# A decoder block's output projection: its weights split into DRAM during the first projection

## The chip, the cores and the metric

The kernel runs on one core of a Trainium2 chip, in float32. The metric is the device time of one launch in microseconds. A core has a matrix engine (TensorE, PE), a vector engine (VectorE, DVE), a scalar engine (ScalarE, ACT), a general engine (GpSimd, POOL) and a sync engine (SyncE, SP), each with its own instruction stream that it works through in order. SP, ACT and POOL issue DMAs. On chip there are SBUF (128 partitions) and PSUM, where matmuls accumulate. The engines wait for each other by semaphores.

## The reference, cut to what matters

One layer over 2048 tokens of width 1024: a norm, one combined projection, stick-breaking attention over 8 heads and gated linear attention (GLA) over 4, head norms, an output projection with a residual, and a feed-forward block (FFN) with a convolution of width 3 and a final norm.

```
h = rms_norm(x, attn_norm_g)
proj = h @ w_in                       # 1024 x 3088
sb_q, sb_k, sb_v, g_q, g_k, g_v, g_lr, g_og = split(proj)
o_sb = head_rms_norm(stick_breaking_attention(sb_q, sb_k, sb_v), sb_out_g)
log_a = log_sigmoid(g_lr @ w_gate_up + b_gate_up) / 16
o_gla = head_rms_norm(gla_chunked(g_q, g_k, g_v, log_a), gla_out_g) * silu(g_og)
x = x + concat([o_sb, o_gla]) @ w_out # 1024 x 1024
h = rms_norm(x, ffn_norm_g)
a, val = split(causal_depthwise_conv(h @ w_ffn_up, conv_w, conv_b))
x = x + (silu(a) * val) @ w_ffn_down
return rms_norm(x, final_norm_g)
```

## The kernel before

The tokens go in four blocks of 512. Every float32 matmul is made of three matmuls in a reduced format: each operand is kept as a high part and a low part (value minus high part), and high x high, high x low and low x high are accumulated. `split_w` (L101) makes the two parts of weights: ACT copies into the high part (L102), POOL or DVE subtracts it for the low part (L103).

The first stage is the projection of the GLA values (`gv_block`, L183) beside the norm of x (`prep`, L193): `prep(b + 1)` and then 4 token tiles of block b, 24 matmuls each. The weights of a projection come in four loads (`load_chunk`, L147) into two buffers `raw` and four pairs `w`. The second stage projects the GLA's queries, keys and gate: for each block the low-rank gate `lr` (two ACT copies, L250 and L251, and one subtract, L252), one matmul with `gu` for each pair of heads (L257) and 24 matmuls for each of the four feature tiles (`mm_feat`, L163). The gate's small operands are loaded in front of it, in L221 to L239. Then follow Q, K, V with the GLA itself, the output gate and attention. Up to the output gate the order of all engines is made by a scheduler with a timeline model of the engines; from there on the order of PE is written out by hand, and the others are scheduled around it.

The output projection and the FFN's down projection run in one generator, `accumulate` (L733): for n = 0, 1 (columns 0 to 511, then 512 to 1023) it takes chunks of 128 rows of the weights, each with 4 token tiles of 3 matmuls (L764 to L766). `load` (L746) brings a chunk: for block 0 a raw 256 KB load by SP, the split, and a 512 KB store of the pair by POOL to DRAM (`wou` for the output projection, `wdn` for the down projection); the later blocks load the pair from there (512 KB). For n = 0 of block 0 it takes its buffers from `ahead` (L690), four raw buffers and four pairs in slots 10, 11 and 14 of the big memory that come free at the end of the attention of the first block; otherwise from `dr`, a ring of three pairs. Beside the first output projection, attention of the next block runs (`z`, `ws`, `acc`), and the first FFN weights come in (`uraw`).

Of the kernel before, what the change touches and what calls it, by code (L numbers as in the profile page):

```python
# [8 lines left out]
F32 = mybir.dt.float32  # L9
F32R = mybir.dt.float32r  # L10
# [40 lines left out]
def hybrid_block_kernel(ctx, tc, x, attn_norm_g, w_in, w_gate_up, b_gate_up, sb_out_g,  # L51
# [60 lines left out]
    def slot(n, shape, dtype, name):  # L112
        return big.tile(shape, dtype, tag=f"slot{n}", name=name)
# [4 lines left out]
    if True:  # L118
# [54 lines left out]
        def mm_tok(w, b, t):  # L173
            ps = mm_ps()
            whi, wlo = w
            ts = slice(t * P, (t + 1) * P)
            for k in range(KT):
                nc.tensor.matmul(ps, hh[b][k // 4][:, k % 4, ts], whi[k], start=(k == 0), stop=False)  # L178
                nc.tensor.matmul(ps, hh[b][k // 4][:, k % 4, ts], wlo[k], start=False, stop=False)  # L179
                nc.tensor.matmul(ps, hl[b][k // 4][:, k % 4, ts], whi[k], start=False, stop=(k == KT - 1))  # L180
            return ps

        def gv_block(w, b):  # L183
            for t in range(4):
                ps = mm_tok(w, b, t)
                gt = ev.tile([P, 2, TB], F32, tag="ev", name="gt")[:, 0]
                nc.scalar.activation(gt, ps, AF.Copy)
                nc.sync.dma_start(out=gvs[b][t * P:(t + 1) * P, :], in_=gt)

        with tc.tile_pool(name="xp", bufs=2, side="right") as xp, tc.tile_pool(name="sm", bufs=2, side="right") as sm:  # L190
            gat = m1_tile([P, D], F32, "gat")

            def prep(b):  # L193
                for t in range(4):
                    xt = xp.tile([P, D], F32, tag="xt", name="xt")
                    r0 = b * TB + t * P
                    nc.sync.dma_start(out=xt, in_=x[r0:r0 + P, :])
                    if r0 == 0:
                        nc.scalar.dma_start(out=gat, in_=attn_norm_g.to_broadcast([P, D]))
                    xn = xp.tile([P, D], F32, tag="xn", name="xn")  # L200
                    ss = sm.tile([P, 1], F32, tag="ss", name="ss")
                    nc.scalar.activation(xn, xt, AF.Square, accum_out=ss)
                    r = rstd_of(sm, ss, D, 1, "n")
                    nc.vector.scalar_tensor_tensor(out=xn, in0=xt, scalar=r, in1=gat, op0=ALU.mult, op1=ALU.mult)
                    for k4 in range(2):
                        tp = pt.tile([P, 4, P], F32, tag="tp", name="tp")
                        for kk in range(4):
                            k = 4 * k4 + kk
                            nc.tensor.transpose(tp[:, kk, :], xn[:, k * P:(k + 1) * P], ident)
                        dh = hh[b][k4][:, :, t * P:(t + 1) * P]  # L210
                        dl = hl[b][k4][:, :, t * P:(t + 1) * P]
                        split_psum(dh, dl, tp)

            prep(0)
            w = load_chunk(OFF_GV)
            for b in range(NB):
                if b + 1 < NB:
                    prep(b + 1)
                gv_block(w, b)

        nc.sync.dma_start(out=bgate, in_=b_gate_up.rearrange("o (j p) -> p (o j)", p=P))  # L221
        nc.sync.dma_start(out=g_o[:, 0:4], in_=sb_out_g.rearrange("o (j p) -> p (o j)", p=P))
        nc.sync.dma_start(out=g_o[:, 4:8], in_=gla_out_g.rearrange("o (j p) -> p (o j)", p=P))


        with tc.tile_pool(name="lr", bufs=2, side="right") as lp, tc.tile_pool(name="lc", bufs=1, side="right") as lc:
            lraw = lc.tile([P, KT, 16], F32, name="lraw")
            nc.sync.dma_start(out=lraw, in_=wv[:, :, OFF_LR:OFF_LR + 16])
            lw = lc.tile([P, KT, 2, 16], F32R, name="lw")
            split_w(lw[:, :, 0, :], lw[:, :, 1, :], lraw)  # L230

            gur = lc.tile([96, 256], F32, name="gur")
            for u in range(6):
                nc.sync.dma_start(out=gur[16 * u:16 * (u + 1), :], in_=w_gate_up)
            gu = lc.tile([96, 256], F32R, name="gu")
            nc.scalar.activation(gu, gur, AF.Copy)
            nc.vector.tensor_tensor(out=gu[64:96, :], in0=gur[64:96, :], in1=gu[64:96, :].bitcast(F32),
                                    op=ALU.subtract)
            mask = lc.tile([P, TB], F32, name="mask")  # L239
            nc.vector.memset(mask, 1.0)  # L240
            nc.vector.memset(mask.rearrange("p (n c) -> p n c", c=P)[:, :, 0:1], 0.0)
            w = load_chunk(OFF_GQK)
            for b in range(NB):
# [11 lines left out]
                for j in range(NPAIR):  # L255
# [38 lines left out]
                    nc.vector.tensor_tensor(out=ee, in0=pk, in1=ee, op=ALU.mult)  # L294
                    nc.sync.dma_start(out=gs[j][b][2], in_=ee)

        cg = ExitStack()
        gl = cg.enter_context(tc.tile_pool(name="gl", bufs=2, side="right"))
        gst = cg.enter_context(tc.tile_pool(name="gst", bufs=1, side="right"))
# [361 lines left out]
    for b in range(NB):  # L661
        for t in range(4):
            if (b, t) == (1, 0):
                tpc = pc.tile([P, 4, 2 * NCH], F32, tag="c", name="tpc")
                for k in range(4):
                    nc.tensor.transpose(tpc[:, k, :], crow[:, k, :], ident[0:2 * NCH, 0:2 * NCH])
                nc.vector.tensor_copy(out=cwb, in_=tpc)
            for part, _ in enumerate(og_group(b, t)):
                if b > 0:

                    if steps < (16 * (b - 1) + 4 * t + part + 1) * FIRST // 46:
                        next(first, None)
                        steps += 1
                    for f, when in enumerate(PAIRS):
                        if f not in oT and steps >= when:
                            oT[f] = o_feat(0, f, pc, "c")
                for f, row in GATED.items():
                    if f not in oT and (b, t) >= row:
                        oT[f] = o_feat(0, f, pc, "c", ot=ots[f % 4])
            if (b, t) == (1, 3):  # L680
                gring.items += gated_rows(0)
                a4 = slot(4, [P, 4, TB], F32, "wtC")
                w45 = slot(5, [P, 2, 2, TB], F32R, "ws45")
                wsr.items += [w45[:, 0], w45[:, 1]]
                ots = [a4[:, k, :].rearrange("p (t q) -> p t q", t=4) for k in range(4)]
            elif (b, t) == (2, 3):
                gring.items += gated_rows(1)
                wraw = slot(11, [P, 4, TB], F32, "wraw")
                wsplit = slot(10, [P, 4, TB], F32R, "wsplit")
    for _ in first:  # L690
        pass
    wmore = slot(14, [P, 4, TB], F32R, "wmore")
    ahead = [Ring([wraw[:, k, :] for k in range(4)]),
             Ring([m[:, 2 * u:2 * u + 2, :] for m in (wsplit, wmore) for u in range(2)])]
    del wsr.items[2:]
    c1.close()
    rings, o2 = later_memory(*shared[:-1], a4, shared[-1])
# [32 lines left out]
            dr.items += [m[:, 2 * u:2 * u + 2, :] for m in spare for u in range(2)]  # L730
        return True

    def accumulate(lhs, w_rows, kept, b, squares=None, extra=None, stagger=False, rstds=None, rows=None, first=None,  # L733
                   final=False):


# [3 lines left out]
        for n in range(2):  # L740
# [4 lines left out]

            def load(ci):  # L746
                at_ = kept[n][rows[ci]]
                pair = first[1].next() if n == 0 and first else dr.next()
                if b > 0:
                    nc.sync.dma_start(out=pair.bitcast(F32), in_=at_.bitcast(F32))  # L750
                else:
                    raw = first[0].next() if n == 0 and first else drr.next()
                    nc.sync.dma_start(out=raw, in_=w_rows[rows[ci] * P:(rows[ci] + 1) * P, ns])
                    split_w(pair[:, 0, :], pair[:, 1, :], raw, nc.vector if first and n == 0 and ci % 2 else nc.gpsimd)
# [62 lines left out]
    def ffn(b, oT, rows, nextT):  # L817
# [15 lines left out]
        if b == 0:  # L833
# [4 lines left out]
        r2 = sm.tile([P, 4], F32, tag="r2", name="r2", bufs=2)  # L838
        rs1, rs2 = ([r[:, t:t + 1] for t in range(4)] for r in (r1, r2))
        last = b + 1 == NB  # L840
        yield from accumulate(oT, w_out, wou, b, squares=sq1, stagger=True, rstds=[r1], rows=rows,
                              extra=previous if b > 0 else remaining, first=None if b > 0 else ahead)
        if b == 0:
            h2h.extend(slot(10 + u, [P, 4, TB], F32R, f"h2h{u}") for u in range(2))
# [24 lines left out]
        for gi, G in enumerate(GROUPS):  # L869
# [53 lines left out]
            yield from accumulate(gts, w_ffn_down[ch0 * P:(ch0 + G) * P, :], [w[ch0:ch0 + G] for w in wdn], b, squares=sq2 if final else None,  # L923
                                  extra=extra, stagger=final and last, rstds=[r2], final=final and last)
            ch0 += G
        while b + 1 < NB and len(nextT) < KT:
# [74 lines left out]
```

## Time and profile before

| | us |
|---|---|
| median of 3 runs | 2754.53 |
| lowest, highest | 2751.18, 2754.88 |
| the profiled execution, whole | 2760.47 |
| its span | 2758.8 |
| PE busy | 2694.3 |
| DVE, ACT, POOL busy | 1685.5, 1147.0, 611.6 |

The profiled execution is one launch of the same program, recorded by the hardware profiler. PE is busy for nearly all of the span, so its order of work is also the order of time: one reads where PE waits, for what, and then what the engine that it waits for was itself waiting for. A row in a timeline begins with the start and the duration, and the bracket at its end says how long the engine was idle before and what ended that.

### The profile page before, as it was taken

To read this page: it belongs to the slowest core of one execution; us is meant where nothing else is said; L and a number is where in the kernel's file an instruction comes from. 1 tells how busy PE (TensorE), PEld (TensorE's weight loads), DVE (VectorE), ACT (ScalarE), POOL (GpSimd) and SP (SyncE) were. 2 spreads that over 40 slices of the span, in tenths; PEclk is the share of its full clock that TensorE was granted. 3 is DMA by queue.
4 is the path that set the end of the run, shared out by engine and by line. 5 is a ranking of instruction groups with operands and counts; after the bars stand their busy time and mean duration, and the time that the engine had idled before them with its cause. 6 is when DMAs were issued, how large, how long until landed. Compare 5 with 4: busy or idle time off the path is not lost.

```text
span 2758.8 us, 36075 instructions
## 1 busy us (share of the span) xinstructions
PE 2694.3 (98%) x13004; PEld 2234.3 (81%) x13004; DVE 1685.5 (61%) x2778; ACT 1147.0 (42%) x2371; POOL 611.6 (22%) x937
## 2 busy tenths in 40 slices
PE   8999999999799999999999999999999999999998
PEld 7878888888688778887888888888888888888887
DVE  5246755467677687876776777777867334242333
ACT  5455533345465455554543444445434222220112
POOL 2001212215555556542111111111110000000000
PEclk9999999999999999999999999999999999999999
DMA  6214644467667677768455555574554656555552
GB/s 191 92 64 173 228 144 156 131 188 242 224 225 257 224 243 255 243 236 274 156 185 181 175 174 174 186 253 152 177 177 150 231 192 221 203 197 191 198 191 84
DMA packets 232169, 526.92 MB, mean 191 GB/s; under 512 B 32294, under 2 KB 120630, under 8 KB 209462
## 3 DMA queue, kind: packets, MB, share of 16 engines
q1 hardware_dynamic: 200742, 387.76, 42.3%
q0 software_dynamic: 31104, 136.33, 13.9%
q8 instruction: 102, 1.67, 0.3%
q14 instruction: 77, 0.63, 0.1%
q10 hardware_dynamic: 144, 0.52, 0.1%
HBM read 382.99 MB, written 141.56 MB: 190 GB/s over the span
## 4 chain that ended last, share of the span: by engine, by line
PE 86%; DVE 5%; DMA 4%; ACT 2%; issue 1%; POOL 1%; SPq 0%; ACTq 0%; POOLq 0%; DVEq 0%
PE ups L886 11%; PE ups L887 11%; PE ups L888 11%; PE d L765 7%; PE d L764 7%; PE d L766 7%; PE z L533 4%; PE tp L566 4%; PE mm L170 2%; PE mm L168 2%; PE mm L169 2%; PE acc L582 2%; PE mm L180 2%; PE mm L179 2%; PE mm L178 2%; PE acc L581 2%
## 5 line engine op out<-in xcount | busy, mean ns | idle before, releaser
L886 PE MATMUL ups<-h2h,u 128*128 128x512 f32 x1408 | 552.2, 392 | 3.9 <-DVE x L791 3.9
L887 PE MATMUL ups<-h2l,u 128*128 128x512 f32 x1408 | 551.1, 391 | 0.0
L888 PE MATMUL ups<-h2h,u 128*128 128x512 f32 x1408 | 550.3, 391 | 0.0
L886 PEld LDWEIGHTS ups<-h2h,u 128*128 128x128 f32 x1408 | 265.2, 188 | 60.6 <-DVE x L791 4.3
L95 DVE TENSOR_TENSOR ws<-tp,ws 128x512 fp32r<-128x512 f32 (+1 forms) x320 | 194.0, 606 | 193.2 <-ACT ws L94 192.3
L888 PEld LDWEIGHTS ups<-h2h,u 128*128 128x128 f32 x1408 | 265.0, 188 | 57.2
L887 PEld LDWEIGHTS ups<-h2l,u 128*128 128x128 f32 x1408 | 265.0, 188 | 55.4
L764 PE MATMUL d<-d,g 128*128 128x512 f32 x736 | 290.4, 395 | 3.8 <-ACT d L102 1.3
L94 ACT ACTIVATE ws<-tp 128x512 fp32r<-128x512 f32 (+1 forms) x320 | 170.3, 532 | 297.0 <-PE tp L566 292.8
L765 PE MATMUL d<-d,g 128*128 128x512 f32 x736 | 288.7, 392 | 1.2 <-POOL d L103 1.2
L766 PE MATMUL d<-d,g 128*128 128x512 f32 x736 | 288.4, 392 | 0.0
L898 DVE SCALAR_TENSOR_TENSOR ct<-ups,cwb,ct 128x511 f32<-128x511 f32 x176 | 131.7, 748 | 249.4 <-POOL ct L897 196.2
L893 ACT ACTIVATE ct<-ups,cwb 128x512 f32<-128x512 f32 x176 | 136.5, 775 | 340.0 <-PE ups L888 339.8
L549 DVE TENSOR_TENSOR_SCAN wtB<-mt,cy 128x512 f32<-128x512 f32 x192 | 249.0, 1297 | 4.4 <-ACT mt L538 4.3
L791 DVE TENSOR_TENSOR x<-d,x 128x512 f32<-128x512 f32 x128 | 85.8, 683 | 164.1 <-PE d L766 164.0
L897 POOL TENSOR_TENSOR ct<-ct,hadd 128x2 f32<-128x2 f32 x132 | 26.7, 202 | 688.5 <-ACT halo L895 324.3
L538 ACT ACTIVATE mt<-z 128x512 f32<-128x512 f32 (+2 forms) x320 | 170.6, 533 | 14.3 <-PE z L536 6.2
L764 PEld LDWEIGHTS d<-d,g 128*128 128x128 f32 x736 | 138.3, 188 | 35.3 <-DVE x L791 2.8
L765 PEld LDWEIGHTS d<-d,g 128*128 128x128 f32 x736 | 138.3, 188 | 31.2 <-POOL d L103 1.8
L766 PEld LDWEIGHTS d<-d,g 128*128 128x128 f32 x736 | 138.2, 188 | 30.8
L168 PE MATMUL mm<-hh,w 128*128 128x512 f32 x384 | 151.3, 394 | 0.0
L170 PE MATMUL mm<-hh,w 128*128 128x512 f32 x384 | 149.3, 392 | 0.9 <-POOL w L103 0.9
(265 smaller groups left out, 5374.2 us busy)
## 6 DMA issues: line engine op xcount, KB each, us to landing
u<-wup SPq DMA_DIRECT2D x132, 1024.0 KB, 4.7
d<-wdn SPq DMA_DIRECT2D x94, 512.0 KB, 3.5
wup<-u POOLq DMA_DIRECT2D x44, 1024.0 KB, 6.6
kvA<-kvs POOLq DMA_DIRECT2D x52, 512.0 KB, 4.6
uraw<-in_w_ffn_up_dram SPq DMA_DIRECT2D x44, 512.0 KB, 4.7
wdn<-d POOLq DMA_DIRECT2D x44, 512.0 KB, 4.9
d<-wou SPq DMA_DIRECT2D x38, 512.0 KB, 4.6
dw<-wdn SPq DMA_DIRECT2D x38, 512.0 KB, 4.3
```

Of the source, the lines that this page charges most:

```text
L94: nc.scalar.activation(hi, ps, AF.Copy)
L95: nc.vector.tensor_tensor(out=lo, in0=ps, in1=hi.bitcast(F32), op=ALU.subtract)
L168: nc.tensor.matmul(ps, whi[k][:, fs], hh[b][k // 4][:, k % 4, :], start=(k == 0), stop=False)
L170: nc.tensor.matmul(ps, wlo[k][:, fs], hh[b][k // 4][:, k % 4, :], start=False, stop=(k == KT - 1))
L538: nc.scalar.activation(m[:, lo:TB], z[:, :width], AF.Sigmoid, scale=-0.125)
L549: nc.vector.tensor_tensor_scan(out=pp[:, ::-1], data0=mr, data1=mr, initial=1.0 if prev is None else prev, op0=ALU.mult, op1=ALU.bypass)
L764: nc.tensor.matmul(accs[t], gh[:, ts], whi, start=(ci == 0), stop=False)
L765: nc.tensor.matmul(accs[t], gh[:, ts], wlo, start=False, stop=False)
L766: nc.tensor.matmul(accs[t], gw[:, ts], whi, start=False, stop=(ci == G - 1))
L886: nc.tensor.matmul(ps, whi[:, k, :], hk, start=(k == 0), stop=False)
L887: nc.tensor.matmul(ps, whi[:, k, :], lk, start=False, stop=False)
L888: nc.tensor.matmul(ps, wlo[:, k, :], hk, start=False, stop=(k == KT - 1))
```

## The change

`gv_block` gets a step of its own for each of its 16 token tiles, `split_ahead`: ACT issues a load of one 128 x 512 piece of `w_out` into `sraw` (a buffer in the tag `n2`, one copy), `split_w` makes the pair in `spair` (a pool `sp` with one buffer), and POOL issues its store into `wou`. The output projection of block 0 then loads pairs from `wou` as the others do: `ahead` becomes a ring of eight pairs in slots 10, 11, 14 and 15, and its own raw loads, splits and stores are gone. The gates' operands (`lraw`, `lw`, `gur`, `gu`, `bgate`, `g_o`) are loaded in the second round of the first stage, into a pool that is opened before it; the mask moves into the pool of the gate's working tiles, which is opened after `sp` is closed. By the addresses that the two programs were given, `spair` has bytes 196608 to 200703 of each partition, and later the mask has 196992 to 199039 and `lr` 199040 to 201087.

```diff
+        def split_ahead(raw, pair, src, dst):
+            nc.scalar.dma_start(out=raw, in_=src)
+            split_w(pair[:, 0, :], pair[:, 1, :], raw)
+            nc.gpsimd.dma_start(out=dst.bitcast(F32), in_=pair.bitcast(F32))
         def gv_block(w, b):
             for t in range(4):
+                i = 4 * b + t
+                split_ahead(n2_tile([P, 512], "sraw"),
+                            sp.tile([P, 2, 512], F32R, tag="spair", name="spair"),
+                            w_out[(i // 2) * P:(i // 2 + 1) * P, (i % 2) * 512:(i % 2 + 1) * 512], wou[i % 2][i // 2])
                 ps = mm_tok(w, b, t)
...
-        with tc.tile_pool(name="xp", bufs=2, side="right") as xp, tc.tile_pool(name="sm", bufs=2, side="right") as sm:
+        lc = cl.enter_context(tc.tile_pool(name="lc", bufs=1, side="right"))
+        lw = lc.tile([P, KT, 2, 16], F32R, name="lw")
...
+        def gate_operands():
+            nc.sync.dma_start(out=lraw, in_=wv[:, :, OFF_LR:OFF_LR + 16])
+            split_w(lw[:, :, 0, :], lw[:, :, 1, :], lraw)
+            for u in range(6):
+                nc.sync.dma_start(out=gur[16 * u:16 * (u + 1), :], in_=w_gate_up)
+            nc.scalar.activation(gu, gur, AF.Copy)
...
+        with tc.tile_pool(name="xp", bufs=2, side="right") as xp, tc.tile_pool(name="sm", bufs=2, side="right") as sm, \
+                tc.tile_pool(name="sp", bufs=1) as sp:
             gat = m1_tile([P, D], F32, "gat")
...
             for b in range(NB):
                 if b + 1 < NB:
                     prep(b + 1)
+                if b == 1:
+                    gate_operands()
                 gv_block(w, b)
-        with tc.tile_pool(name="lr", bufs=2, side="right") as lp, tc.tile_pool(name="lc", bufs=1, side="right") as lc:
-            lraw = lc.tile([P, KT, 16], F32, name="lraw")
...
-            mask = lc.tile([P, TB], F32, name="mask")
+        with tc.tile_pool(name="lr", bufs=2, side="right") as lp:
+            mask = lp.tile([P, TB], F32, tag="mask", name="mask", bufs=1)
...
-                wraw = slot(11, [P, 4, TB], F32, "wraw")
-                wsplit = slot(10, [P, 4, TB], F32R, "wsplit")
+                wsplit = [slot(n, [P, 4, TB], F32R, f"ws{n}") for n in (10, 11)]
     for _ in first:
         pass
-    wmore = slot(14, [P, 4, TB], F32R, "wmore")
-    ahead = [Ring([wraw[:, k, :] for k in range(4)]),
-             Ring([m[:, 2 * u:2 * u + 2, :] for m in (wsplit, wmore) for u in range(2)])]
+    wsplit += [slot(n, [P, 4, TB], F32R, f"ws{n}") for n in (14, 15)]
+    ahead = Ring([m[:, 2 * u:2 * u + 2, :] for m in wsplit for u in range(2)])
...
-                pair = first[1].next() if n == 0 and first else dr.next()
-                if b > 0:
+                pair = first.next() if n == 0 and first else dr.next()
+                if split:
                     nc.sync.dma_start(out=pair.bitcast(F32), in_=at_.bitcast(F32))
                 else:
-                    raw = first[0].next() if n == 0 and first else drr.next()
+                    raw = drr.next()
...
-        yield from accumulate(oT, w_out, wou, b, squares=sq1, stagger=True, rstds=[r1], rows=rows,
+        yield from accumulate(oT, w_out, wou, True, squares=sq1, stagger=True, rstds=[r1], rows=rows,
```

The order of ACT where the first projection ends and the second begins, before (`gt` is a result of `gv_block`, `w` a weight pair of the second projection; a name such as DMAHW2 or DMASW7 is a semaphore that DMAs count on, DMASW for those that POOL issues):

```order
L187 ACTIVATE gt_1097<-mm_1072 128x512 [waits DMAHW7_49,PE_49,Activation_49]
L102 ACTIVATE w_1159<-raw_1157 128x1024 [waits PE_49]
L102 ACTIVATE w_1164<-raw_1162 128x1024 [waits PE_49]
L187 ACTIVATE gt_1125<-mm_1100 128x512 [waits DMAHW0_49,PE_49,Activation_49]
L102 ACTIVATE w_1169<-raw_1167 128x1024 [waits DMAHW2_49]
L250 ACTIVATE lr_1194<-mm_1177 32x512 [waits DVE_49,PE_49]
L251 ACTIVATE lr_1194<-mm_1177 32x512
L102 ACTIVATE w_1174<-raw_1172 128x1024 [waits DMAHW3_49]
```

The same place of ACT now, from the last result of the first projection on:

```order
L197 ACTIVATE gt_1245<-mm_1220 128x512 [waits DMAHW5_49,PE_49]
L185 DMA sraw_1180<-in_w_out_dram 128x512 [waits Pool_49]
L102 ACTIVATE w_1269<-raw_1267 128x1024 [waits DMAHW0_49]
L102 ACTIVATE w_1274<-raw_1272 128x1024 [waits DMAHW1_49]
L102 ACTIVATE spair_1181<-sraw_1180 128x512 [waits DMAHW3_49,DMASW5_49]
L185 DMA sraw_1214<-in_w_out_dram 128x512 [waits Pool_49]
L102 ACTIVATE spair_1215<-sraw_1214 128x512 [waits DMAHW6_49,DMASW6_49]
L267 ACTIVATE lr_1294<-mm_1277 32x512 [waits DVE_49,DMASW7_49,PE_49,Pool_49]
L268 ACTIVATE lr_1294<-mm_1277 32x512
```

The last two of the 16 split steps stand between `w_1274` and `lr` (L267 is what was L250), and `lr` also waits for DMASW7, the store of the last pair.

The order of PE there, before (`mm_1198` is the first feature tile of block 0, 24 matmuls; L257 the gate's):

```order
L168 MATMUL mm_1198<-hh0_1_261,w_1169 128x512 [waits Activation_49]
L169 MATMUL mm_1198<-hl0_1_263,w_1169 128x512
L257 MATMUL mm_1223<-lr_1194,gu_1151 128x512 [waits DMAHW3_49,DMAHW4_49,DMAHW2_49,DMAHW5_49,DMAHW1_49,DMAHW6_49,DMAHW0_49,DMAHW7_49,DVE_49,PE_49]
L168 MATMUL mm_1244<-hh0_0_260,w_1159 128x512
L169 MATMUL mm_1244<-hl0_0_262,w_1159 128x512
```

And now (`mm_1298` is that feature tile, L274 the gate's matmul):

```order
L168 MATMUL mm_1298<-hh0_1_261,w_1274 128x512 [waits Activation_49]
L169 MATMUL mm_1298<-hl0_1_263,w_1274 128x512
L170 MATMUL mm_1298<-hh0_1_261,w_1274 128x512 [waits DVE_49]
L168 MATMUL mm_1298<-hh0_1_261,w_1274 128x512
L169 MATMUL mm_1298<-hl0_1_263,w_1274 128x512
L170 MATMUL mm_1298<-hh0_1_261,w_1274 128x512
L274 MATMUL mm_1323<-lr_1294,gu_272 128x512 [waits DMASW7_49,DMASW6_49,DMAHW0_49,DMASW5_49,DMAHW1_49,DMASW4_49,DMAHW2_49,DMASW3_49,DMAHW3_49,DMASW2_49,DMAHW4_49,DMASW1_49,DMAHW5_49,DMASW0_49,DMAHW6_49,DVE_49,DMAHW7_49,PE_49,Pool_49]
L168 MATMUL mm_1344<-hh0_0_260,w_1259 128x512
```

The gate's matmul stood after 14 of the 24 matmuls of that tile; now it stands after all 24.

The order of ACT at the first output projection, before (`mt`, `wtA` and `wtB` belong to attention of the next block, `u2` is the high part of FFN weights, `g1_0` an operand of the output projection):

```order
L538 ACTIVATE mt1_5035<-z_6353 128x512
L540 ACTIVATE wtA_5065<-z_6353 128x512
L102 ACTIVATE wmore_6281<-wraw_5978 128x512
L102 ACTIVATE u2_6308<-uraw_7107 128x1024
L102 ACTIVATE wmore_6281<-wraw_5978 128x512
L97 ACTIVATE g1_0_5976<-tpo_6471,g_o_70 128x512
L538 ACTIVATE mt0_5034<-z_6479 128x512
```

And now:

```order
L556 ACTIVATE mt1_5135<-z_6454 128x512
L558 ACTIVATE wtA_5165<-z_6454 128x512
L102 ACTIVATE u2_6409<-uraw_7160 128x1024
L97 ACTIVATE g1_0_6076<-tpo_6554,g_o_70 128x512
L556 ACTIVATE mt0_5134<-z_6562 128x512
L558 ACTIVATE wtB_5166<-z_6562 128x512
```

The two copies into `wmore` around `u2` are gone; `g1_0` still follows `u2`.

## Rows read from the trace of the kernel before

**Rows 1.** The page: span, and busy us, share and count of each engine.

```profile
span 2758.8 us, 36075 instructions
PE 2694.3 (98%) x13004; PEld 2234.3 (81%) x13004; DVE 1685.5 (61%) x2778; ACT 1147.0 (42%) x2371; POOL 611.6 (22%) x937
```

**Rows 2.** Waits of PE: who waited for whom, us in total, times, longest.

```profile
PE tp L209 <- DVE xn L204: 11.1, 2, 9.5
...
PE d L764 <- ACT wmore L102: 5.5, 1, 5.5
PE d L765 <- POOL wmore L103: 3.3, 1, 3.3
...
PE d L765 <- POOL wsplit L103: 0.8, 1, 0.8
```

**Rows 3.** Timeline of PE, 688 to 712 us: start, duration, line, operation [idle before].

```profile
688.70 0.39 PE L764 MATMUL d<-wsplit,g 128*128 128x512 f32 x1
689.92 0.50 PE L765 MATMUL d<-wsplit,g 128*128 128x512 f32 x1 [0.84 <-POOL wsplit L103]
...
695.63 0.71 PE L533 MATMUL z<-kvA,qA 128*128 128x512 f32 x2
701.84 0.80 PE L764 MATMUL d<-wmore,g 128*128 128x512 f32 x1 [5.49 <-ACT wmore L102]
705.90 0.79 PE L765 MATMUL d<-wmore,g 128*128 128x512 f32 x1 [3.27 <-POOL wmore L103]
...
711.88 0.40 PE L764 MATMUL d<-wmore,g 128*128 128x512 f32 x1
```

**Rows 4.** Timeline of ACT at the same place.

```profile
700.21 1.06 ACT L102 ACTIVATE u<-uraw 128x1024 fp32r<-128x1024 f32 x1 [8.62 <-DMA uraw<-in_w_ffn_up_dram]
...
701.69 0.67 ACT L97 ACTIVATE g<-tpo,g_o 128x512 fp32r<-128x512 f32 x1
```

**Rows 5.** Timeline of PE in columns 512 to 1023 of that projection.

```profile
733.39 0.40 PE L766 MATMUL d<-d,g 128*128 128x512 f32 x1
735.10 0.50 PE L764 MATMUL d<-d,g 128*128 128x512 f32 x1 [1.31 <-ACT d L102]
736.46 0.50 PE L765 MATMUL d<-d,g 128*128 128x512 f32 x1 [0.85 <-POOL d L103]
```

**Rows 6.** Timeline where the first projection ends, all engines.

```profile
119.81 0.40 PE L168 MATMUL mm<-hh,w 128*128 128x512 f32 x1
...
120.98 0.59 ACT L251 ACTIVATE lr<-mm 32x512 fp32r<-32x512 f32 x1
...
121.60 0.68 DVE L252 TENSOR_TENSOR lr<-mm,lr 32x512 fp32r<-32x512 f32 x1 [4.77 <-ACT lr L251]
...
122.28 1.06 ACT L102 ACTIVATE w<-raw 128x1024 fp32r<-128x1024 f32 x1 [0.71 <-DMA raw<-in_w_in_dram]
...
123.02 0.40 PE L257 MATMUL mm<-lr,gu 96*128 96x512 f32 x1
```

**Rows 7.** Timeline at the start.

```profile
10.17 2.36 POOL L103 TENSOR_TENSOR w<-raw,w 128x1024 fp32r<-128x1024 f32 x1
```

**Rows 8.** Windows: length, busy PE, PEld, DVE, ACT, POOL; granted clock, DMA share, GB/s.

```profile
695.00:700.00 5.00, 1.35 (x8) 0.78 (x7) 0.59 (x1) 0.00 (x0) 0.00 (x0) 1.00 1.03 405
705.00:710.00 5.00, 4.10 (x10) 3.23 (x11) 1.39 (x1) 0.00 (x0) 1.90 (x3) 0.50 0.96 354
120.00:130.00 10.00, 10.00 (x45) 8.20 (x44) 5.62 (x7) 9.03 (x13) 2.40 (x1) 1.00 0.47 149
```

**Rows 9.** Operations on tile `draw`: ns min/median/max, first and last start.

```profile
L102 ACT ACTIVATE d<-draw x52: 615/632/644, 670.9 to 1253.6; 128x512 fp32r<-128x512 f32 x52
L103 POOL TENSOR_TENSOR d<-draw,d x52: 1264/1297/1888, 671.6 to 1254.3; 128x512 fp32r<-128x512 f32 x52
```

**Rows 10.** L755, the stores of split weights to `wou` and `wdn`.

```profile
DMA to landing us min/median/max: 3.5/5.3/10.5
```

**Rows 11.** The page's DMA issues: count, KB each, median us to landing.

```profile
kvA<-kvs POOLq DMA_DIRECT2D x52, 512.0 KB, 4.6
```

More of the change, by code (lines that the diff above doesn't have):

```diff
@@ L188, in gv_block @@
                 nc.sync.dma_start(out=gvs[b][t * P:(t + 1) * P, :], in_=gt)
-        with tc.tile_pool(name="xp", bufs=2, side="right") as xp, tc.tile_pool(name="sm", bufs=2, side="right") as sm:
+        cl = ExitStack()
+        lc = cl.enter_context(tc.tile_pool(name="lc", bufs=1, side="right"))
+        lw = lc.tile([P, KT, 2, 16], F32R, name="lw")
+        gu = lc.tile([96, 256], F32R, name="gu")
+        lraw = lc.tile([P, KT, 16], F32, name="lraw")
+        gur = lc.tile([96, 256], F32, name="gur")
+        def gate_operands():
[4 more added lines that the diff above has]
+            nc.scalar.activation(gu, gur, AF.Copy)
+            nc.vector.tensor_tensor(out=gu[64:96, :], in0=gur[64:96, :], in1=gu[64:96, :].bitcast(F32),
+                                    op=ALU.subtract)
+            nc.sync.dma_start(out=bgate, in_=b_gate_up.rearrange("o (j p) -> p (o j)", p=P))
+            nc.sync.dma_start(out=g_o[:, 0:4], in_=sb_out_g.rearrange("o (j p) -> p (o j)", p=P))
+            nc.sync.dma_start(out=g_o[:, 4:8], in_=gla_out_g.rearrange("o (j p) -> p (o j)", p=P))
+        with tc.tile_pool(name="xp", bufs=2, side="right") as xp, tc.tile_pool(name="sm", bufs=2, side="right") as sm, \
+                tc.tile_pool(name="sp", bufs=1) as sp:
             gat = m1_tile([P, D], F32, "gat")
@@ L218, in hybrid_block_kernel @@
                     prep(b + 1)
+                if b == 1:
+                    gate_operands()
                 gv_block(w, b)
-        nc.sync.dma_start(out=bgate, in_=b_gate_up.rearrange("o (j p) -> p (o j)", p=P))
-        nc.sync.dma_start(out=g_o[:, 0:4], in_=sb_out_g.rearrange("o (j p) -> p (o j)", p=P))
-        nc.sync.dma_start(out=g_o[:, 4:8], in_=gla_out_g.rearrange("o (j p) -> p (o j)", p=P))
-        with tc.tile_pool(name="lr", bufs=2, side="right") as lp, tc.tile_pool(name="lc", bufs=1, side="right") as lc:
-            lraw = lc.tile([P, KT, 16], F32, name="lraw")
[L228 to L238, printed above, removed]
-            mask = lc.tile([P, TB], F32, name="mask")
+        with tc.tile_pool(name="lr", bufs=2, side="right") as lp:
+            mask = lp.tile([P, TB], F32, tag="mask", name="mask", bufs=1)
             nc.vector.memset(mask, 1.0)
@@ L295, in hybrid_block_kernel @@
                     nc.sync.dma_start(out=gs[j][b][2], in_=ee)
+        cl.close()
         cg = ExitStack()
@@ L731, in after_attention, with accumulate @@
         return True
-    def accumulate(lhs, w_rows, kept, b, squares=None, extra=None, stagger=False, rstds=None, rows=None, first=None,
+    def accumulate(lhs, w_rows, kept, split, squares=None, extra=None, stagger=False, rstds=None, rows=None, first=None,
                    final=False):
@@ L747, in load @@
                 at_ = kept[n][rows[ci]]
-                pair = first[1].next() if n == 0 and first else dr.next()
-                if b > 0:
+                pair = first.next() if n == 0 and first else dr.next()
+                if split:
                     nc.sync.dma_start(out=pair.bitcast(F32), in_=at_.bitcast(F32))
                 else:
-                    raw = first[0].next() if n == 0 and first else drr.next()
+                    raw = drr.next()
                     nc.sync.dma_start(out=raw, in_=w_rows[rows[ci] * P:(rows[ci] + 1) * P, ns])
-                    split_w(pair[:, 0, :], pair[:, 1, :], raw, nc.vector if first and n == 0 and ci % 2 else nc.gpsimd)
+                    split_w(pair[:, 0, :], pair[:, 1, :], raw)
                     nc.gpsimd.dma_start(out=at_.bitcast(F32), in_=pair.bitcast(F32))
@@ L922, in extra @@
                         nextT.append(o_feat(b + 1, len(nextT), *((pc, "c") if done == total else (pz, "z"))))
-            yield from accumulate(gts, w_ffn_down[ch0 * P:(ch0 + G) * P, :], [w[ch0:ch0 + G] for w in wdn], b, squares=sq2 if final else None,
+            yield from accumulate(gts, w_ffn_down[ch0 * P:(ch0 + G) * P, :], [w[ch0:ch0 + G] for w in wdn], b > 0, squares=sq2 if final else None,
                                   extra=extra, stagger=final and last, rstds=[r2], final=final and last)
```

## The prediction

> **What bounds the kernel now.** I read the busy table first: TensorE (PE) is busy 2694.3 of 2758.8 us [rows 1], so it is the bound nearly everywhere and only its gaps, some 64 us, can be won, or added to. Next the waits of PE [rows 2]: apart from the start (`tp` on `xn`, 11.1 us) the longest that one stage has are at the first output projection, on `wmore` and `wsplit`, the split pairs of `w_out`: 5.5, 3.3 and 0.8 us. Then the timelines around these [rows 3 to 5], and around the two places where the change puts new work: the end of the first projection [rows 6] and the start [rows 7]. PE's step between two 512-column matmuls is read there too: 14 of them go from 119.81 to 123.02, 0.229 us each [rows 6].
>
> **1. First output projection, columns 0 to 511: what goes.** Losses are taken from start to start, less what PE executes between. From 688.70 to 689.92 one matmul: 1.22 - 0.23 = 0.99. From 695.63, after two `z`, to 701.84: 6.21 - 0.46 = 5.75. From 701.84 to 705.90: 4.06 - 0.23 = 3.83 [rows 3]. After that the granted clock is 0.50 (1.2 GHz) in 705 to 710, where it was 1.00 in 695 to 700, in which PE had worked only 1.35 of 5 us [rows 8]. Eleven matmuls, four small transposes and two `z` take from 705.90 to 711.88, 5.98 us [rows 3]; at full clock 11 x 0.23 + 2 x 0.23 + 4 x 0.11 = 3.4, so 2.6 are lost to the clock. Sum 13.1 us.
>
> Is the cause removed? The row that waits on ACT is `wmore`'s, but ACT itself stands before `u<-uraw` for 8.62 us, until 700.21, for a load of FFN weights [rows 4], while the DMA engines are full: 1.03 of their share, 405 GB/s [rows 8]. So the wait is a queue of bytes. The change takes 8 stores of 512 KB out of this stretch and makes 8 loads of 256 KB into 8 of 512 KB, four of which go into memory that is free well before. By the order of issues, what is moved from about 670 us to this load falls from 11.7 to 6.75 MB; 5 MB at 405 GB/s are 12 us, of which I count on 7 to 9: it lands near 692. No `wmore` stands behind it on ACT any more (its order there, below the diff); `g1_0` does, an operand of a late chunk. I take the whole 13.1; if `g1_0` is still held up there, 3 to 6 of them come back (rival C).
>
> **2. The same projection, columns 512 to 1023.** Before, PE lost 1.48 at 735.10 and 1.13 at 736.46 [rows 5], 2.6 in all, waiting on split work. After, a buffer of the ring of three is refilled by one 512 KB load: 4.6 us from issue to landing for a like transfer [rows 11], where a 256 KB load, 0.63 us on ACT and 1.30 on POOL [rows 9] stood. A chunk of 12 matmuls lasts 2.7 us, so three buffers nearly cover it. I expect a loss of 1.3 to 3.5, middle 2.3: -0.3 net, -1.3 to +0.9.
>
> **3. The end of the first projection: what is added.** This is the term that decides. Sixteen split tiles run in a chain with one `sraw` and one `spair`: the ScalarE copy of a tile waits for the store of the one before, POOL's subtract follows, then a POOL-issued 512 KB store. The schedule puts the last two copies (`spair_1181`, `spair_1215`) on ACT behind `w_1274`, the last weights of the next projection, and behind both of them `lr`, the gate's low-rank result, with a wait on DMASW7: `lr` and the mask lie in memory that `spair` had, so `lr` waits until the last store has landed. Before, `lr` followed the matmuls alone and was there in time: PE had no wait at L257, at 123.02 [rows 6].
>
> The chain: `w` is split from 122.28 for 1.06 us, held until there by its own load [rows 6], which the change does not advance: 123.34. A copy of 0.63 and a subtract of 1.30 [rows 9]: 125.27. A store S: 125.27 + S. Copy and subtract again: 127.20 + S; a store again: 127.20 + 2S. Then the two ACT copies of `lr`, 0.59 each, and VectorE's 0.68 [rows 6], and some 0.05 for each of seven hand-overs (121.57 to 121.60 for one): the gate's matmul can start at 129.4 + 2S. PE reaches it, which now stands behind all 24 matmuls of `mm_1298`, at 119.81 + 24 x 0.229 = 125.3. Everything of PE in this stage stands behind it in order, and PE has nothing else.
>
> S is not in the trace at this place. From above: stores of split weights take 5.3 us in the middle, from full stretches [rows 10]; stall 129.4 + 10.6 - 125.3 = 14.7. From below: 3.5, the shortest of them: 11.1. The DMA engines are at 0.47 in 120 to 130 [rows 8], so I stay nearer to the short end: S = 4.0, stall 12.1. Nothing in PE's order could fill it. After a wait half as long the clock fell to 0.50 for 5 us (part 1), so 2.5 more: 14.6 us; bounds 11 (no fall) and 18 (14.7 plus 3). A price that a page gives, apart from the sum: the rows have 3.5 to 5.3 and 4.6 us for POOL-issued transfers of 512 KB [rows 10, 11]; the Trainium skill's page DMA: Bandwidth & Descriptors, section "Anatomy of one DMA — SWDGE (gpsimd) path", states 2.0 us plus bytes over 436e3 per us, an estimate of 3.2 here. By that the stall would be 10.5 and the total 1.6 lower than mine; every row lies above it.
>
> **4. The start.** Two `w_out` tiles join the loads that PE's first matmuls wait for. ACT copies `spair_499` (0.63) before it copies `hh`; POOL subtracts (1.30) and issues the store before the 2.36 us subtract of `w`, which began at 10.17 [rows 7] and which the third matmul of the first tile needs. The first `tp` waits for 9.5 us [rows 2], for x and the norm's weights, with the new load behind them on ACT's queue. Bounds 0 (the x loads decide as before) and 2.5 (all three items in a row); I take 1.0. Later in this stage a tile has 24 x 0.229 = 5.5 us of PE for 0.63 us of ACT and 1.30 of POOL; POOL is 22% busy over the span [rows 1], so it is covered.
>
> **5. The gates' operands.** A dozen small loads and copies move some 90 us ahead. They were early already where it matters (no PE wait at L257), so 0. The work removed from ACT and POOL at the output projection is counted in parts 1 and 2; as busy time it was and is beside PE.
>
> **Sum.** -13.1 - 0.3 + 14.6 + 1.0 = +2.2 on the profiled execution's 2760.47, so 2762.7; that execution is 5.9 above the median of the runs, 2754.53, so 2757 in the terms of these.
>
> **The rivals.** A: *faster, the transition costs less*. If only one of the two stores is still ahead when `w` has been split, because the copy of the last tile but one slips in while ACT waits for `w`'s load, `lr` is late by one copy, subtract and store less: 129.4 + 4.0 - 1.93 - 125.3 = 6.2, with little fall of the clock 7. With part 1 whole and 0.5 at the start: -13.1 - 0.3 + 7 + 0.5 = -5.9: 2749, and 2748 with S = 3.5. For it: the DMA engines are half idle there [rows 8]. Against it: the order on ACT has `spair_1181` behind `w_1274`, and its load holds it to 122.28 [rows 6].
> B: *slower, the chain is long*. The place is the same `lr`: with S = 5.3 the stall is 14.7 and the clock takes 3; if the start takes 2 as well, 19.7 stand against 13.4: +6.3, 2761, and up to +12 (2766) if the chain also delays the loads of `w`. With the start at 2 it decides from S of about 5.2 on, where the sum passes +5.5. For it: 5.3 is the middle of the stores' row [rows 10]. Against it: they come from stretches with fuller DMA engines.
> C: *slower, the uraw load still gates ACT at the output projection*. `g1_0` stands behind `u2` on ACT, so if that load lands at 697 or later PE waits 3 to 6 us there and the clock falls again: +5 to +9, 2760 to 2763. For it: the DMA engines were full for a quarter of the stage; against: 5 MB fewer in front.
> D: *the change does nothing*: no stall at the transition because the wait is met, and PE bound by g1_0 as before: it falls inside the forecast's range.
>
> **How the numbers follow.** A measurement of this kernel tells 0.2%, 5.5 us, from no change. The forecast (with D), -4 to +5.5, has 0.54; A 0.15; B 0.20; C 0.11. So faster 0.15, same 0.54, slower 0.31. The likeliest case's own range is 2750 to 2760; the bounds of part 3 (11 to 18) and part 4 (0 to 2.5) widen it upward, A's upper half downward: 2748 to 2767.
>
> **What would show it.** Right: a PE wait of 11 to 13 us on `lr` (L274) near 126 us with ACT waiting on a DMA just before `lr`, granted clock 0.50 in the slices behind it, no wait on a split pair at 688 to 712, ACT's `u2<-uraw` before 695, and a load instead of a split behind PE's waits of the columns 512 to 1023. Wrong: no PE wait at L274 (A), stores of 5 us or more (B), or a PE wait on `g` after 690 (C). The forecast as such falls if the total differs by more than 5.5 us from before.

## The result, and the profile after

The change makes the kernel slower: 2773.72 us median of 4 runs (2772.6 to 2775.49) against 2754.70 (2751.18 to 2759.22), a ratio of 1.0062 with a 95% interval of 1.0043 to 1.0082. The forecast was 2757, range 2748 to 2767.

The page of the changed kernel, span and busy times, which answer to [rows 1]:

```profile
span 2772.1 us, 36109 instructions
PE 2698.3 (97%) x13004; PEld 2236.6 (81%) x13004; DVE 1682.3 (61%) x2774; ACT 1146.5 (41%) x2371; POOL 613.8 (22%) x941
```

Its waits of PE (who for whom, us in total, times, longest), which answer to [rows 2]:

```profile
PE tp L240 <- DVE xn L235: 14.0, 5, 10.0
PE mm L274 <- DVE lr L269: 12.7, 1, 12.7
...
PE d L780 <- DMA d<-wou: 2.1, 2, 1.1
PE mm L168 <- ACT w L102: 1.9, 1, 1.9
...
PE z L551 <- DVE g L98: 1.6, 1, 1.6
```

No split pair of `w_out` is waited for at columns 0 to 511 any more. What is new stands in four places: `xn` in five waits instead of two, `lr`, `w`, and, at the output projection, `g` and the pairs from DRAM.

Where the time went is read best by holding the same matmul against itself in both traces. The table gives its start in the changed kernel less its start in the profiled execution of before, at some points of that one:

| at, us | after | after, 2nd profile | what lies in between |
|---|---|---|---|
| 84 | +4.1 | +2.9 | first projection |
| 124.4 | +7.1 | +6.0 | late weights `w` of the second |
| 128 | +22.3 | +20.1 | `lr`, and the slow clock behind it |
| 682 | +21.2 | +19.0 | |
| 710.3 | +8.5 | +6.3 | output projection, columns 0 to 511 |
| 715.4 | +11.9 | +9.6 | the wait on `g`, then on `x` |
| 737 | +11.8 | +9.5 | columns 512 to 1023 |
| 2700 | +13.4 | +14.1 | |

The end of the first projection, timeline of ACT in the changed kernel, which answers to [rows 6]:

```profile
119.66 0.63 ACT L102 ACTIVATE spair<-sraw 128x512 fp32r<-128x512 f32 x1 [2.25 <-DMA wou<-spair]
120.19 1.04 ACT L102 ACTIVATE w<-raw 128x1024 fp32r<-128x1024 f32 x1
...
129.07 1.06 ACT L102 ACTIVATE w<-raw 128x1024 fp32r<-128x1024 f32 x1 [4.54 <-DMA raw<-in_w_in_dram]
130.04 0.61 ACT L102 ACTIVATE spair<-sraw 128x512 fp32r<-128x512 f32 x1
...
138.00 0.63 ACT L102 ACTIVATE spair<-sraw 128x512 fp32r<-128x512 f32 x1 [7.35 <-DMA wou<-spair]
143.26 0.59 ACT L267 ACTIVATE lr<-mm 32x512 fp32r<-32x512 f32 x1 [4.63 <-DMA wou<-spair]
```

The chain of the last two stores is there as forecast: copy at 130.04, the next at 138.00 when the first store has landed, `lr` at 143.26 when the second has. But `w` is split at 129.07, where it was 122.28. Of the 6.8 us, 4.1 come from the first projection; the rest begins at 119.66, where ACT had waited 2.25 us for an earlier store before it could split the `w` that frees a buffer for this load. POOL issued the two last stores here (its timeline):

```profile
132.83 0.57 POOL L187 DMA_DIRECT2D wou<-spair  x1 [0.30 <-POOL spair L103]
...
140.27 0.57 POOL L187 DMA_DIRECT2D wou<-spair  x1 [0.30 <-POOL spair L103]
```

PE there, and two windows (busy PE, PEld, DVE, ACT, POOL; granted clock, DMA share, GB/s):

```profile
130.19 0.50 PE L168 MATMUL mm<-hh,w 128*128 128x512 f32 x1 [1.94 <-ACT w L102]
...
145.37 0.77 PE L274 MATMUL mm<-lr,gu 96*128 96x512 f32 x1 [12.71 <-DVE lr L269]
```

```profile
130.00:140.00 10.00, 1.94 (x6) 0.97 (x6) 1.23 (x1) 1.28 (x3) 3.62 (x3) 0.83 0.44 149
140.00:150.00 10.00, 4.63 (x11) 3.74 (x12) 2.88 (x6) 4.92 (x7) 0.57 (x1) 0.50 0.13 52
```

The wait is 12.7 us; 12.1 had been worked out. After it the granted clock is 0.50 (1.2 GHz), and PE falls 2.3 us further behind.

The output projection, timelines of SP and of ACT in the changed kernel, the second of which answers to [rows 4], and then of PE:

```profile
692.36 0.80 SPq L766 DMA_DIRECT2D d<-wou  x2
...
694.53 1.01 SPq L766 DMA_DIRECT2D ws<-wou  x2
...
697.17 1.28 SPq L766 DMA_DIRECT2D ws<-wou  x2
699.48 0.38 SPq L896 DMA_DIRECT2D uraw<-in_w_ffn_up_dram  x1
```

```profile
718.81 1.06 ACT L102 ACTIVATE u<-uraw 128x1024 fp32r<-128x1024 f32 x1 [13.60 <-DMA uraw<-in_w_ffn_up_dram]
719.77 0.67 ACT L97 ACTIVATE g<-tpo,g_o 128x512 fp32r<-128x512 f32 x1
```

```profile
721.28 0.73 PE L551 MATMUL z<-kvA,qA 128*128 128x512 f32 x2 [1.64 <-DVE g L98]
...
725.45 0.50 PE L780 MATMUL d<-d,g 128*128 128x512 f32 x1 [0.70 <-DVE x L807]
...
727.22 0.50 PE L780 MATMUL d<-d,g 128*128 128x512 f32 x1 [0.81 <-DVE x L807]
...
738.79 0.50 PE L780 MATMUL d<-d,g 128*128 128x512 f32 x1 [0.92 <-DMA d<-wou]
...
747.95 0.50 PE L780 MATMUL d<-d,g 128*128 128x512 f32 x1 [1.15 <-DMA d<-wou]
```

The load of FFN weights still lands late, at 718.8; without the 21.2 by which the stage is shifted, that is 697.6. It was issued at 699.48, so 19.3 us before; the windows from 700 to 705 and from 710 to 715 have a DMA share of 1.05 and 1.01. `g`'s copy stands behind it on ACT, and that, with a wait on `x` behind it, costs 3.4 us by the table.

What held the load is in the rows of SP: six pairs of `w_out`, 512 KB each, were issued in the 7.1 us before it. By the packets of the trace (this kind of load alone moves pieces of 512 bytes on SP's queue), its first piece was started 15.4 us after the issue, and in these 15.4 us 4.0 MB were started on SP's queue and 2.1 MB on POOL's. Windows of the whole stretch, from where 670 us of before is to the landing, in the kernel before and in the changed one (columns as above; the second number is the length, the last GB/s):

```profile
670.00:700.20 30.20, 24.73 (x112) 19.55 (x110) 18.11 (x22) 10.62 (x21) 23.06 (x30) 1.00 1.01 372
```

```profile
691.20:718.80 27.60, 27.03 (x124) 22.09 (x124) 11.90 (x19) 6.62 (x14) 11.66 (x17) 1.00 1.01 366
```

That is 11.2 MB before and 10.1 MB now.

### The profile page after: what moved, and what is told of

Same layout as the page of the kernel before. It is cut to its first block, busy times and chain, and to the rows that moved or that the text cites. A ratio compares the mean times of both kernels' runs of the same rounds, so it can differ in the third digit from the quotient of the medians.

```text
span 2772.1 us, 36109 instructions
## 1 busy us (share of the span) xinstructions
PE 2698.3 (97%) x13004; PEld 2236.6 (81%) x13004; DVE 1682.3 (61%) x2774; ACT 1146.5 (41%) x2371; POOL 613.8 (22%) x941
## 4 chain that ended last, share of the span: by engine, by line
PE 68%; DVE 3%; DMA 1%; POOL 1%; ACT 0%; issue 0%; SPq 0%; ACTq 0%; POOLq 0%; DVEq 0%
PE ups L902 11%; PE ups L903 11%; PE ups L904 11%; PE d L780 7%; PE d L781 7%; PE d L782 7%; PE z L551 4%; PE tp L584 4%; PE acc L600 2%; PE acc L599 2%; PE tpu L872 1%; DVE wtB L567 1%; DVE x L807 1%; DVE ws L95 0%; DVE ohp L621 0%
```

## The experiments

Two theories. **T**: the cost is the chain of split steps through one buffer (it holds `lr`, ACT and thereby `w`), and the gain at the output projection is smaller than 13 because those 13 were one execution's. **R**: the cost is the bytes, 4 MB of loads and 8 MB of stores beside the first projection, or the moved gate operands; and the 13 are fixed by the program's order.

| kernel | median, us | ratio to before, 95% |
|---|---|---|
| before again | 2757.02 | 0.9999 (0.9981 to 1.0016) |
| change again | 2773.33 | 1.0060 (1.0039 to 1.0080) |
| `lr` apart | 2764.28 | 1.0035 (1.0018 to 1.0051) |
| two half buffers | 2755.51 | 0.9994 (0.9981 to 1.0006) |
| gate operands alone | 2757.82 | 1.0003 (0.9987 to 1.0020) |
| change, third FFN tile on POOL | 2771.06 | 1.0051 (1.0033 to 1.0069) |
| before, output projection freed of that load | 2751.89 | 0.9984 (0.9970 to 0.9997) |
| half buffers, third FFN tile on POOL | 2751.80 | 0.9984 (0.9971 to 0.9996) |
| the same, `lr` apart | 2752.71 | 0.9992 (0.9979 to 1.0005) |
| the same, half of `w_out` early | 2753.42 | 0.9992 (0.9979 to 1.0005) |

**The kernel before, profiled again, three times, unchanged.**

> The kernel before, unchanged, profiled a second time: its first profiled execution was 2760.5 us, 5.8 above the median of its runs. If the gain of the change at the first output projection is overstated by that one execution (theory A), the waits on wmore there are shorter in this one by about 6 us in all and the execution lies near 2754. If those waits are fixed by the order of the program (theory B), they come out at 5.5, 3.3 and 0.8 us again and the 6 us lie elsewhere.

> The kernel before, unchanged, a third profile. Of two so far the third FFN load landed at 700 (13.1 us lost at the first output projection) and at 691 (3 us lost); with the gates' operands moved it landed at 692. Theory (the late landing is the rare case): it lands at 690 to 694 again and PE waits under 3 us for wmore there. Rival (both are common): 697 or later and over 6 us.

> The same once more, a fourth profile of the kernel before, with the same two forecasts: under 3 us of waits for wmore, or over 6.

Timeline of ACT in the second profile (span 2749.4), which answers to [rows 4]:

```profile
690.34 0.63 ACT L102 ACTIVATE wmore<-wraw 128x512 fp32r<-128x512 f32 x1
691.15 1.06 ACT L102 ACTIVATE u<-uraw 128x1024 fp32r<-128x1024 f32 x1 [0.18 <-DMA uraw<-in_w_ffn_up_dram]
692.11 0.62 ACT L102 ACTIVATE wmore<-wraw 128x512 fp32r<-128x512 f32 x1
```

Timelines of ACT in the third (span 2761.0) and in the fourth (span 2749.8):

```profile
690.87 0.63 ACT L102 ACTIVATE wmore<-wraw 128x512 fp32r<-128x512 f32 x1
700.94 1.06 ACT L102 ACTIVATE u<-uraw 128x1024 fp32r<-128x1024 f32 x1 [9.43 <-DMA uraw<-in_w_ffn_up_dram]
```

```profile
692.30 1.06 ACT L102 ACTIVATE u<-uraw 128x1024 fp32r<-128x1024 f32 x1 [0.32 <-DMA uraw<-in_w_ffn_up_dram]
```

The waits of PE for `wmore` in the third, and in the fourth:

```profile
PE d L764 <- ACT wmore L102: 6.3, 1, 6.3
PE d L765 <- POOL wmore L103: 3.3, 1, 3.3
```

```profile
PE d L765 <- POOL wmore L103: 1.6, 1, 1.6
```

The same program has the load ready for ACT at 700.2, 691.2, 700.9 and 692.3, and the execution took 2760.5, 2751.1, 2762.7 and 2751.5 us. From 682 to 710 the second and the fourth are 9.6 and 9.7 us faster than the first, so that they lose some 3 us where it lost 13; the third is 0.9 slower. So the prediction's largest term of gain was one of two cases, and each was met twice in four. The rare-case theory fell with the third profile.

The load was issued at much the same time in all four, here in the first and the second (timeline of SP; the row holds this load and the next, 2.1 us later):

```profile
681.56 4.47 SPq L880 DMA_DIRECT2D uraw<-in_w_ffn_up_dram  x2
```

```profile
680.93 3.90 SPq L880 DMA_DIRECT2D uraw<-in_w_ffn_up_dram  x2
```

So it was under way for 18.6, 10.2, 19.5 and 10.3 us, and POOL's DMAs around it stand at the same distance from its issue to 0.03 us. What differs is in the packets: of the 2048 pieces of 512 bytes of these two loads, 419, 939, 458 and 846 had been started 8 us after the issue, while two queues were sending at some 400 GB/s. Why the DMA engines took more of them in two of the executions is open. The changed kernel has no such two cases in what was recorded: its load landed at 697.6 and 697.5, shifts taken off, and its eight runs lie within 3 us (2772.55 to 2775.49), where those of the kernel before lie within 19.

**The change, profiled again.**

> The change itself, profiled a second time. Theory (the waits on lr and on w are fixed by the program's order and by the length of the chain, and the loss at the first output projection moves with one FFN load): the wait at L274 is again 11 to 14 us, and the total again 2770 to 2776. Rival (the first profile caught a rare case at the transition, as that of before did at the output projection): the wait at L274 differs by more than 4 us.

It came out as the theory said: a wait of 11.5 us at L274, and the second column of the table. The transition is no chance: it stands in both profiles, and all eight runs of the change are above 2772.

**`lr` and the mask in other memory.**

```diff
+        sp = cl.enter_context(tc.tile_pool(name="sp", bufs=1))
...
-                tc.tile_pool(name="sp", bufs=1) as sp:
...
-            mask = lp.tile([P, TB], F32, tag="mask", name="mask", bufs=1)
+            ml = m1_tile([P, 2, TB], F32R, "ml")
+            mask = ml[:, 0, :].bitcast(F32)
+            lr = ml[0:96, 1, :]
...
-                lr = lp.tile([96, TB], F32R, tag="lr", name="lr", bufs=1)
```

> The change with lr and the mask in memory that the norm's weights had (free by then), and the buffer of the split pairs kept to the end of the second projection, so that nothing of the second projection waits for the last store. Theory (lr waits for the chain of the last two stores): the wait of 12.7 us at L274 and the slow clock behind it, 2 to 3, go: 15 us less than the change, about 2759. Rival (the load on the DMA engines and on ACT makes the second projection late, whatever lr's memory): PE waits a like time for w or for other work there, and the total falls by less than 5, above 2768.

2764.28: between the two, and neither came out. Nothing waits for the last store now, and the second projection still starts late; PE's timeline there:

```profile
125.89 0.50 PE L170 MATMUL mm<-hh,w 128*128 128x512 f32 x1 [1.42 <-POOL w L103]
...
132.47 0.80 PE L168 MATMUL mm<-hh,w 128*128 128x512 f32 x1 [4.03 <-ACT w L102]
...
134.26 0.79 PE L275 MATMUL mm<-ml,gu 96*128 96x512 f32 x1 [0.57 <-DVE ml L270]
```

The shift at 128 us is +13.3 in place of +22.3: with `lr` in other memory 9 us go. Behind it stand the weights, which are later here than in the change (+12.6 already at 124.4, where the change has +7.1), because the order on ACT came out differently with this edit: the first of the two `w` that free the buffers stands behind one more copy that waits for a store (timeline of ACT).

```profile
121.50 0.63 ACT L102 ACTIVATE spair<-sraw 128x512 fp32r<-128x512 f32 x1 [3.16 <-DMA wou<-spair]
122.04 1.99 ACT L102 ACTIVATE w<-raw 128x1024 fp32r<-128x1024 f32 x2
```

In the change they were split at 116.34 and 120.19. So the 9 us are a net, and this run alone does not divide the cost between the memory and the order on ACT.

**Two half-size buffers** (the raw piece comes in halves too).

```diff
...
+            for u in range(2):
+                us = slice(u * 256, (u + 1) * 256)
+                pair = sp.tile([P, 2, 256], F32R, tag="spair", name="spair", bufs=2)
+                nc.scalar.dma_start(out=raw[:, us], in_=src[:, us])
+                split_w(pair[:, 0, :], pair[:, 1, :], raw[:, us])
+                nc.gpsimd.dma_start(out=dst[:, :, us].bitcast(F32), in_=pair.bitcast(F32))
...
```

> The change with two buffers of half the size (128 x 256 pieces) in place of one, same bytes and same memory: a store has to be over only when the second next copy begins. Theory (the single buffer makes a chain of 6.3 us for each tile, beside 5.5 us of matmuls, and ACT stands in it): PE's waits on xn, 3.7 us, and on w, 3, go, and the wait on lr falls below 3 us: 2752 to 2757. Rival (the bytes of the loads and stores are the load): the waits on xn and on w stay, the total falls by less than 8: above 2765.

2755.51, the time of before: 18 us less than the change, with the same bytes. PE reaches the gate's matmul without a wait:

```profile
124.80 0.40 PE L277 MATMUL mm<-lr,gu 96*128 96x512 f32 x1
```

and its shift at 128 us is +1.8. So the transition is the chain's, not the bytes'. What the first projection costs is less clear. At 86 us the shift is +1.8, +5.5 and +1.4 in the three profiles with half buffers and all of `w_out`, the +5.5 from the slowest of that version's 12 runs; it is +0.6 with only half of `w_out` split early, +1.0 with the gate operands alone, and +0.1 to +0.5 in the kernel before, profiled again. The change has +4.1 and +2.9, two kernels made from it +4.0 and +6.5. With one profile each these overlap, and no run here separates the bytes from the buffer or the split work in that stage.

**The gate operands alone**, moved as in the change, in the kernel before.

> The kernel before with the gates' operands alone moved into the second round of the first projection, and no early split of w_out. Theory (that part costs nothing): within 4 us of the kernel before, 2751 to 2758, and the waits at the output projection as before. Rival (the moved loads and the copy of gu between the norms make PE's waits on xn longer): 3 us or more at xn, 2757 to 2760.

1.0003 (0.9987 to 1.0020): this part costs nothing that can be told.

**The third FFN tile on POOL**, in the change:

```diff
+                        if (c, s) == (1, 0):
+                            nc.gpsimd.tensor_copy(out=whi, in_=raw)
+                            nc.gpsimd.tensor_tensor(out=wlo, in0=raw, in1=whi.bitcast(F32), op=ALU.subtract)
+                        else:
+                            split_w(whi, wlo, raw)
```

> The change with both parts of the third FFN weight tile made on POOL, so that no copy that waits for its load stands on ACT ahead of g1_0. Theory (g1_0 stands behind that load, 3.6 us of PE between 718 and 722): these go, about 2770. Rival (PE would wait for the next thing, x or POOL's masks, as long): no difference, 2773.

The stretch from 710 to 715 loses 0.5 where it lost 3.4, near what the theory says, so 2.9 of the 3.4 hung on that copy; the total, 2771.06, is lower by about as much, but its interval overlaps that of the change.

**The kernel before with the same edit, and the low part of the seventh of eight chunks on DVE** (the last that POOL made).

```diff
-                    split_w(pair[:, 0, :], pair[:, 1, :], raw, nc.vector if first and n == 0 and ci % 2 else nc.gpsimd)
+                    split_w(pair[:, 0, :], pair[:, 1, :], raw, nc.vector if first and n == 0 and (ci % 2 or ci > 5) else nc.gpsimd)
```

> The kernel before with the same edit, and the low part of the last chunk of w_out made on DVE: nothing of the output projection stands behind the third FFN load any more, but every byte, raw load, split and store is still there. Theory (what PE lost there, 13.1 us in one execution and 2.8 in another, is this one load landing at 700 or at 691): no wait on wmore of over 1 us, and the total 4 to 8 us below before, 2747 to 2751. Rival (the loss is the raw loads' own lateness in the full queue): PE waits for wmore a like time, through its raw load, and the total stays at 2755.

2751.89, by 0.16% below before, with an interval that ends just under 1. The load landed late in this execution, and POOL waited for it (POOL's timeline):

```profile
698.49 1.25 POOL L882 CAST u<-uraw 128x1024 fp32r<-128x1024 f32 x1 [6.04 <-DMA uraw<-in_w_ffn_up_dram]
```

PE had no wait on `wmore` at all, with every load, split and store in its place; it lost 2.5 us on `x` instead:

```profile
PE d L764 <- DVE x L791: 2.5, 1, 2.5
```

So what PE lost there was the order on ACT and POOL behind one late load, not the split work that the change took away; this rests on one profile and on the total.

**Versions.**

> The change with two half-size buffers (the kernel that came out at the time of before) and the third FFN weight tile on POOL. Theory: 3.6 us of the 4.7 that it loses in the output projection's second part go, 2751 to 2752, faster than before by 3 to 4. Rival: the waits on x and on the pairs from DRAM take their place, 2755.

> The version with half-size buffers and the third FFN weight tile on POOL, and lr and the mask also out of the pairs' memory. Theory (with two half buffers the last store is over before lr needs its memory): no difference to the version without, 2752. Rival (1.8 us that the version with half buffers loses at the start of the second projection are this memory): 2750.

> As the version with half-size buffers and the third FFN weight tile on POOL, but only the eight pieces of w_out for the columns 0 to 511 are split early, beside the second and third block of the first projection; the other eight are split where they were before. Theory (the early split costs in the first stage, where it stands beside the norms and the first loads; its gain is in the columns 0 to 511): half the cost in the first stage, no wait at the start or on lr, the gain kept: 2748 to 2751. Rival (the norms' waits come with any early split, and the raw path of the second half loses its 2.6 us again): 2753 to 2756.

The first has both edits above, half buffers and the third FFN tile on POOL: 0.9984 (0.9971 to 0.9996), well below the change and just below before. The second is the first with `lr` apart; the third is the first with only the columns 0 to 511 split early (beside tiles 4 to 11). Neither is told from the first, or from before, and the third's theory (2748 to 2751) did not come out: 2753.42. The small edit of before without any early split is as fast as the best of them.

## Why the prediction was wrong

The forecast was no change; it came out 0.6% slower, outside the range. Each step:

- **Part 1 failed, in size and in cause.** "I take the whole 13.1": in the first profile the stretch did lose 13.1 and the changed kernel 12.7 less, so read against that profile the term holds. But two of four executions lose some 3 us there, so the mean loss of these is 8.5 ((13.1 + 3.5 + 14.0 + 3.4) / 4, each from the first by the difference at 710 less that at 682). The change still loses 0.4 there, so its gain against the four is 8.1. The working had seen that the loss hung on one load in a full queue and did not ask whether it would land at the same time twice. The landing "near 692" was wrong too, 697.6 in these terms, and with it the count of bytes behind it: from about 670 us to this load 6.75 MB had been expected in place of 11.7. The kernel before moved 11.2 MB there in its first profile and 7.7 in its second, the changed one 10.1: POOL's queue fell from 6.5 MB in the first to 3.2, and SP's rose from 4.7 to 7.0, with the pairs of `w_out` ahead of this load.
- **Rival C came with it**, at 3.4 us, 2.9 of which went when the copy was moved: `g1_0` behind the late load. It had 0.11 and was set against the forecast as an alternative; it can stand beside any other case, and did.
- **Part 2**: expected a loss of 2.3, measured 0.92 and 1.15 on the pairs from DRAM, 2.1; net -0.1 from 715 to 737. Right.
- **Part 3 was right in its mechanism and its main size** (12.1 forecast, 12.7 and 11.5 measured; the clock 2.5, measured 2.3). It failed in one clause: `w` is split from 122.28, "which the change does not advance". The change delays it, by 6.8 us; 4.1 of these come from the first projection, and PE loses 3.0 more here (4.1 to 7.1 in the table), because a copy that waits for a store stands on ACT ahead of the earlier `w`. That had been named, as the reason for rival B's upper end, and left out of the sum. The stores took 5.2 us (issued at 132.83, landed by 138.00) and 3.0 (140.27 to 143.26), 8.2 together where twice 4.0 had been taken. From the Trainium skill's page DMA: Bandwidth & Descriptors, section "Anatomy of one DMA — SWDGE (gpsimd) path", 3.2 us had been estimated for this size. The second store, with a DMA share of 0.13, is near that; the first, with other transfers beside it (0.44), is not.
- **Part 4 failed**: 1.0 forecast for the start and 0 for the rest of the first projection ("so it is covered"), 4.1 and 2.9 measured. The start is not where it went: the first `tp` comes 0.5 and 0.1 us later than before. It went in the part put at nothing, in four waits on `xn` between 24 and 67 us, 4.0 and 2.6 us together. The cover was judged by the busy time of ACT and POOL; what came late were the loads of x. ACT stood idle for them 7 times, 17.6 us in all, up to 95 us; before it was 3 times, 4.8 us. They took 5.2 us in the middle from issue to landing, before 3.9. Whether the transfers beside them did it, or buffers that came free later, is not shown. The view of the tile `xt` in that window has both for the changed kernel (us, times; then us):

```profile
  DMA xt<-in_x_dram: 17.6, 7
...
DMA to landing us min/median/max: 3.2/5.2/7.3
```

- **Part 5** was right as far as can be told: the gate operands alone gave 1.0003.

The sum by these: 20.1 (19.0 to 21.2 at 682 us) at the front, where 15.6 had been forecast, and -8.1 + 3.4 - 0.1 = -4.8 at the output projection, where -13.4 had been: +15.3. Some 2 to 4 us of the 17 to 19 measured lie in small differences later, such as 2.0 and 2.2 us between 2300 and 2395, and are not traced further.

## What to carry to other kernels

A loss that hangs on one transfer in a full queue is not a property of the program: look at a second execution before a gain is built on it, and spread between runs (2747 to 2766 for this kernel) is a hint that there may be two. Work that is put "beside" another stage through a single buffer stands on an in-order engine, and its wait for a store delays whatever is queued behind it: count its time per step (6.1 to 6.8 us here from 81 to 120 us) against that of the stage (5.5 us), and look at what takes over its memory. When a stall is read from an engine that waits for a load, first take the waiting instruction out of the queue ahead of the critical one; that was worth as much here as moving all the work.

## What the runs showed of the hardware

- The same load, in the same program, issued at the same distance from its neighbours, landed 10.2 to 19.5 us after its issue in different executions when two queues kept the DMA engines at 1.0 of their share.
- A load of 512 KB on SP's queue behind six others of that size had its first piece started 15.4 us after its issue (15.0 in the second profile).
- A POOL-issued store of 512 KB landed in 5.2 us beside other transfers and in 3.0 us nearly alone.
- POOL's cast of a 128x1024 tile took 1.25 us, its subtract of the same tile 2.39, in the kernel before with that edit.
